# Four pairs of column groups as seven block products, spread over the head groups, the merge gates and the first branch

## The chip, the cores and the metric

The kernel runs on one core of one Trainium2 chip. The metric is the device time of one execution in microseconds (us), lower is better; three runs of the kernel before have a median of 1148.04 us.

## The reference

One decoder layer over 256 tokens of width 2048: a combined input projection, two token mixers side by side (gated linear attention, and differential attention with 16 heads), a gated merge of the two branches, and an output projection with a residual.

```python
h = rmsnorm(x, pre_norm_g)                       # x: (256, 2048)
(a_q, a_k, a_v, a_g, a_lr, b_q, b_k, b_v, b_g, m_a, m_b) = split(h @ w_in)
...
y_a = (rmsnorm(o_a, gla_norm_g) * silu(a_g)) @ w_branch_a      # gated linear attention
y_b = (rmsnorm(o_b, diff_norm_g) * 0.8 * silu(b_g)) @ w_branch_b   # differential attention
merged = sigmoid(m_a) * y_a + sigmoid(m_b) * y_b
out = x + rmsnorm(merged @ w_out, post_norm_g)
```

All of it is float32. b_g, m_a and m_b are 2048 columns each of the one wide matrix w_in.

## The kernel before

**Precision.** Every float32 weight and activation is split into two float32r parts, hi and lo. A product is three matmuls on TensorE (PE): hi by hi, lo by hi, hi by lo. ScalarE (ACT) makes hi, VectorE (DVE) makes lo.

**Chunks and units.** The weights are cut into chunks with keys: v, k, q, ag for the linear attention; dv, bg, dq, dk of head groups 0 to 3 (four heads each); m0g and m1g, the merge gates of the branches in groups of 512 columns; y0g and y1g, the branch products; o, the output. `chunk_plan` gives their order in DRAM. A token-major chunk of 512 columns has eight units of 128 x 1024 weights, a unit being twelve matmuls of 512 columns. A channel-major chunk (k, q, dq, dk) has two units. Two units come with one load of 1 MB into a `raw` tile (three buffers), issued on SyncE's queue (SP).

**The stream of units.** `schedule` writes out the order of all units. `emit_half` loads and splits the next unit (hi and lo have three buffers each), `take` hands one to the matmuls and keeps the emission AHEAD = 4 units in front. Side work (the attention of the heads, the preparation of operands) is written as generators that `pump` advances between units. A planner then orders each engine's instructions by their place in the program and by when it reckons them ready, and hands out buffers as they come free.

**Buffers.** The pool `big` has 34 tiles of 4 KB per partition, behind `u(...)`: xs (8, the split activations), oah/oal (8, the linear attention's output), per head group dv, ub, obh, obl and three tiles for each pair of heads, the merge gates (8). `t2` is a ring of eight tiles of 2 KB, PSUM has eight banks. `away` makes a DRAM tile.

**The sets.** m0 is not computed as four plain groups but as two sets. A set takes two groups of 512 columns as a 2 x 2 matrix of blocks and the tokens by halves of the width, and needs seven block products in place of eight (a form of Strassen's scheme). `PRODUCTS` lists them: the operand of the tokens, and the weight block that is loaded. Sums of weight blocks are made by the loads: two chains of four tiles each, a block loaded into a chain plainly first, and later ones added by an accumulating load issued on Pool's queue (GpSimd). Only the fourth product, a12, has its block unsummed; it goes through a `raw` tile (raw_s). `block_operands` makes the sums of the tokens' blocks, `start_sets` issues the first eight chain loads, and each emitted block issues the load of the one eight later (`load_block`). A block is six matmuls of 512 columns.

**Order before.** After the linear attention: heads 0, heads 1, y0 (its results, part, go to DRAM), heads 2, heads 3, then the stage in which the 56 blocks of the two sets run between the 32 units of m1, then y1, merge and o. obh and obl, the heads' results, go to DRAM as they are made and are reloaded with part ahead of y1 on SP's queue.

Of the kernel before, what the change touches and what calls it, by code (L numbers as in the profile page):

```python
# [30 lines left out]
def chunk_plan():  # L31
# [31 lines left out]

    heads(0)
    heads(1)
    for g in range(4):
        branch(0, g)
    heads(2)
    heads(3)
    for g in range(4):  # L70
        gate(1, g)
    for g in range(4):
        branch(1, g)
    for g in range(4):
        gate(0, g)
    for g in range(4):
# [8 lines left out]
def schedule():  # L85

    kinds = {key: kind for key, kind, _, _ in chunk_plan()}
    steps = []

    def regular(*keys):  # L90
        steps.extend((key, n) for key in keys for n in range(units(kinds[key])))

    def mixed(sets, *keys):
        s = [(i, n) for i in sets for n in range(SLOTS * 4)]
        at = len(steps)
        regular(*keys)
        r = steps[at:]
        del steps[at:]
        i = j = 0
        while i < len(s) or j < len(r):  # L100
            if j == len(r) or (i < len(s) and i * len(r) <= j * len(s)):
                steps.append(s[i])
                i += 1
            else:
                steps.append(r[j])
                j += 1

    order = [key for key, _, _, _ in chunk_plan()]
    first = order.index("m10")
    regular(*order[:first])  # L110
    mixed((0, 1), *(f"m1{g}" for g in range(4)))
    regular(*(f"y1{g}" for g in range(4)), *(f"o{g}" for g in range(4)))
    return steps


SLOTS = 7
SETS = (("m00", "m01"), ("m02", "m03"))

# [13 lines left out]
def hybrid_kernel(ctx: ExitStack, tc, xt, xn, preg, postg, w, w2, gkb, glag, lamv, diffg, ident_d, causal_d, lmask_d, out):  # L132
# [46 lines left out]
    raws = {}  # L179
    chains = [[], []]  # L180
    set_steps = [step for step in steps if not isinstance(step[0], str)]

# [15 lines left out]
    def load_block(i):  # L198
        if i < len(set_steps):
            chain, src, adds = block_unit(i)  # L200
            if adds:
                pool.dma_start(chain, src, accum_op=ALU.add)
            elif chain is not None:
                sp.dma_start(chain, src)

    def emit_half():
        j = emitted[0]
        emitted[0] += 1
        key, unit = steps[j]
        if isinstance(key, int):  # L210
            i = set_steps.index((key, unit))
            raw, src, _ = block_unit(i)
            if raw is None:
                h = unit % 2
                g = PRODUCTS[unit // 4][2][1]
                if h == 0:
                    kh = PRODUCTS[unit // 4][2][0]
                    raws[key] = wpool.tile([P, 2048], F32, tag="raw", name=f"raw_s{key}_{unit}")
                    sp.dma_start(raws[key], piece(SETS[key][g], 2 * kh + (unit % 4) // 2))
# [3 lines left out]
            act.activation(hi_t, raw, AF.Copy)  # L223
            dve.tensor_tensor(out=lo_t, in0=raw, in1=f32(hi_t), op=ALU.subtract)  # L224
            load_block(i + 8)
            ready[j] = ((key, unit), hi_t, lo_t)
            return
# [38 lines left out]
    used = [0]  # L266

    def take(key):
# [135 lines left out]
    def token_major(key, n, ops, step=1, groups=1):  # L404
        run = token_steps(key, n, ops, step, groups)
        while True:
            try:
                next(run)
            except StopIteration as e:
                return e.value  # L410

    def token_steps(key, n, ops, step=1, groups=1):
        banks = [[ps(tag), ps(tag)] for tag in ("mm", "bg")[:groups]]
        spots = [(g, b) for g in range(groups) for b in range(2)]
        rows = 2 // groups
        for q in range(KT // rows):
# [16 lines left out]
            if groups == 2 and q > 10:  # L433
                pump()
            if q < KT // rows - 1:
                yield
        return banks if groups == 2 else banks[0]
# [219 lines left out]
    oah = [u([P, 2, 2, S], "oah", F32R) for _ in range(4)]  # L657
    oal = [u([P, 2, 2, S], "oal", F32R) for _ in range(4)]

    def gla_out(hf, gates):  # L660
# [22 lines left out]
        for j in range(4):  # L683
# [41 lines left out]
    def diff_scores(g, pair, h, q2, kh, kl, vv, uu):  # L725
# [22 lines left out]
        return {"g": g, "pair": pair, "h": h, "z": z, "prob": prob, "vv": vv, "uu": uu}  # L748

# [23 lines left out]
    def normed(s, og):  # L773
# [10 lines left out]
        for b in range(2):  # L784
            dve.scalar_tensor_tensor(out=og[:, s["h"] % 2, b, :], in0=bank[:, P * b : P * b + P], scalar=e[:, b : b + 1], in1=s["uu"][:, b, hv], op0=ALU.mult, op1=ALU.mult)

    def diff_attention():
# [3 lines left out]
        while n < 16 or last or pair:  # L791
            new = None
            if n < 16:
# [8 lines left out]
                yield  # L802
                turn_weights(new)
            if last:
                weigh(last)
# [27 lines left out]

    def diff_heads(g, before_pair=lambda pair: None):
# [4 lines left out]
        banks = token_major(f"bg{g}", 512, x_ops, 2)  # L839
        uu = u([P, 2, 512], "ub")  # L840
        for b in range(2):
            gate(banks[b], b, uu[:, b, :])
        obh.append(u([P, 4, S], "obh", F32R))
        obl.append(u([P, 4, S], "obl", F32R))
        for pair in range(2):
            before_pair(pair)
            ts = []
# [58 lines left out]

    def start_sets():
        for c in range(2):
            chains[c].extend(u([P, 1024], f"chain{c}") for _ in range(4))
        for i in range(8):  # L910
            load_block(i)

    def block_set(n, use):
# [54 lines left out]
        yield  # L968

    tasks.append(diff_attention())  # L970
    diff_heads(0)
    diff_heads(1)

    while not {"out0", "out1"} <= done:
        pump()
    part_far = [away([P, 2, 512], "part_far") for _ in range(4)]
    for g in range(4):
        banks = token_major(f"y0{g}", 512, a_ops, 2)
        t = u([P, 2, 512], "part")
        for b in range(2):  # L980
            act.activation(t[:, b, :], banks[b], AF.Copy)
        pool.dma_start(part_far[g], t)

    diff_heads(2)
    operands = block_operands()
    tasks.append(operands)
    diff_heads(3, lambda pair: start_sets() if pair else None)

    while "squares" not in done:
        with tc.issue_after(latest[0]):  # L990
            next(operands, None)
    gates = [[None] * 4, [None] * 4]

    def merge_gate(br, g, b, src):
        if gates[br][g] is None:
            gates[br][g] = u([P, 2, 512], "mgate")
        act.activation(gates[br][g][:, b, :], src, AF.Tanh, scale=half_rstd[:, b : b + 1])

    def set_gates():
        for n in range(2):  # L1000
            yield from block_set(n, lambda src, i, b: merge_gate(0, 2 * n + i, b, src))

    def group_gates():
        for g in range(4):
            banks = yield from token_steps(f"m1{g}", 512, x_ops, 2)
            for b in range(2):
                merge_gate(1, g, b, banks[b])
            yield

    lanes = {True: set_gates(), False: group_gates()}  # L1010
    at = used[0]
    for key, _ in steps[at : at + 56 + 32]:
        next(lanes[isinstance(key, int)])
    for lane in lanes.values():
        assert next(lane, DONE) is DONE
    while tasks:
        pump()
    obh = [u([P, 4, S], "obh", F32R) for _ in range(4)]
    obl = [u([P, 4, S], "obl", F32R) for _ in range(4)]
    part = [u([P, 2, 512], "part") for _ in range(4)]  # L1020
    for g in range(4):
        sp.dma_start(f32(obh[g]), obh_far[g])
        sp.dma_start(f32(obl[g]), obl_far[g])
    for g in range(4):
        sp.dma_start(part[g], part_far[g])
    mh = [u([P, 4, S], "mh", F32R) for _ in range(4)]
    ml = [u([P, 4, S], "ml", F32R) for _ in range(4)]
# [156 lines left out]
```

## Time and profile before

| | before |
|---|---|
| median of 3 runs | 1148.04 us (1147.26 to 1149.27) |
| profiled execution, its own time | 1150.09 us |
| its span | 1148.3 us |
| PE busy | 1125.1 us, 98%, 5650 matmuls recorded |
| DVE, ACT, Pool busy | 748.3, 635.6, 84.1 us |
| moved by the DMA queues | 236.77 MB, 206 GB/s |

Times count from the start of the span. "Busy" is the time in which an engine executed; a matmul's recorded duration overlaps its successor's. In rows of the timeline the bracket gives the idle time ahead of an instruction and what ended it. "Granted clock" (PEclk) is the share of PE's full clock. The DMA share is the mean busy share of the core's 16 DMA engines; it can come out a little above 1. "SPq" is SyncE's queue, where loads are issued in order.

### The profile page before, as it was taken

What the parts mean: (1) busy time and instruction counts of PE and PEld (TensorE: products, weight loads), DVE (VectorE), ACT (ScalarE), POOL (GpSimd) and SP (SyncE); (2) the same over time, 40 slices, a digit from 0 to 9 for tenths busy, and PEclk for the clock granted to TensorE, in tenths of its full rate; (3) what the DMA queues carried; (4) which work ended last, traced back from release to release, by engine and by line L of the source; (5) the groups of instructions that cost most, each with busy time, mean ns of one, the idle gap of its engine ahead of it and who ended that gap; (6) DMA issues with size and microseconds to landing.
All of it is one profiled execution on the core that took longest, in us unless ns stands there. A gap on an engine that the chain in (4) does not pass through costs nothing.

```text
span 1148.3 us, 14907 instructions
## 1 busy us (share of the span) xinstructions
PE 1125.1 (98%) x5650; PEld 966.7 (84%) x5650; DVE 748.3 (65%) x1081; ACT 635.6 (55%) x942; POOL 84.1 (7%) x105
## 2 busy tenths in 40 slices
PE   9999999999999999999999999999899899999997
PEld 9999888888888888888888888888788787887886
DVE  6765587657847766775444677788677576655454
ACT  7675454445646665675444575477666464443441
POOL 0100031001100000000000010003112010000000
PEclk9999999999999999999999999999999899999999
DMA  8756555545454454456665555858899969657552
GB/s 310 228 191 220 184 177 176 196 167 195 141 175 168 151 180 155 177 187 221 221 215 183 184 187 180 307 188 226 254 304 262 257 183 365 209 195 257 187 216 74
DMA packets 41383, 236.77 MB, mean 206 GB/s; under 512 B 5152, under 2 KB 5792, under 8 KB 20320
## 3 DMA queue, kind: packets, MB, share of 16 engines
q1 hardware_dynamic: 34256, 211.70, 52.0%
q0 software_dynamic: 6336, 23.07, 9.1%
q10 hardware_dynamic: 720, 1.06, 0.3%
q8 instruction: 44, 0.72, 0.3%
q14 instruction: 27, 0.22, 0.1%
HBM read 227.42 MB, written 8.39 MB: 205 GB/s over the span
## 4 chain that ended last, share of the span: by engine, by line
PE 89%; DMA 3%; ACT 2%; DVE 2%; issue 2%; POOL 0%; SPq 0%; DVEq 0%; POOLq 0%; ACTq 0%
PE mm L426 55%; PE mm L449 15%; PE mm L451 7%; PE set L930 5%; PE bg L426 2%; DMA raw_m<-in_w_dram 1%; DMA raw_y<-in_w_dram 1%; PE mm L401 1%; PE bg L618 1%; ACT hi L262 1%; DVE lo L263 1%; PE bg L401 1%; PE bg L736 1%; DMA obl<-obl_far 1%; PE bg L737 1%
## 5 line engine op out<-in xcount | busy, mean ns | idle before, releaser
L426 PE MATMUL mm<-hi,xs 128*128 128x512 f32 (+2 forms) x1280 | 312.0, 385 | 7.5 <-ACT hi L262 7.5
L426 PEld LDWEIGHTS mm<-hi,xs 128*128 128x128 f32 x1280 | 239.7, 189 | 48.0 <-ACT hi L262 8.6
L449 PE MATMUL mm<-xs,hi 128*128 128x512 f32 x768 | 195.6, 393 | 0.0
L426 PE MATMUL mm<-lo,xs 128*128 128x512 f32 (+2 forms) x640 | 168.5, 383 | 0.0
L449 PEld LDWEIGHTS mm<-xs,hi 128*128 128x128 f32 x768 | 138.5, 189 | 24.2
L426 PEld LDWEIGHTS mm<-lo,xs 128*128 128x128 f32 x640 | 120.6, 189 | 20.8 <-DVE lo L263 0.3
L263 DVE TENSOR_TENSOR lo<-raw_y,hi 128x1024 fp32r<-128x1024 f32 x64 | 78.1, 1225 | 63.2 <-ACT hi L262 62.6
L262 ACT ACTIVATE hi<-raw_y 128x1024 fp32r<-128x1024 f32 x64 | 67.6, 1060 | 88.8 <-PE mm L426 77.3
L451 PEld LDWEIGHTS mm<-xs,lo 128*128 128x128 f32 x768 | 104.8, 190 | 7.5
L451 PE MATMUL mm<-xs,lo 128*128 128x256 f32 x768 | 107.1, 282 | 0.0
L224 DVE TENSOR_TENSOR lo<-chain,hi 128x1024 fp32r<-128x1024 f32 x48 | 58.6, 1223 | 17.8 <-ACT hi L223 17.1
L223 ACT ACTIVATE hi<-chain 128x1024 fp32r<-128x1024 f32 x48 | 50.8, 1061 | 27.9 <-PE set L930 19.4
L263 DVE TENSOR_TENSOR lo<-raw_bg,hi 128x1024 fp32r<-128x1024 f32 x32 | 39.2, 1224 | 30.8 <-ACT hi L262 30.8
L263 DVE TENSOR_TENSOR lo<-raw_ag,hi 128x1024 fp32r<-128x1024 f32 x32 | 41.2, 1289 | 27.2 <-ACT hi L262 27.2
L263 DVE TENSOR_TENSOR lo<-raw_m,hi 128x1024 fp32r<-128x1024 f32 x32 | 39.1, 1223 | 28.2 <-ACT hi L262 27.9
L262 ACT ACTIVATE hi<-raw_ag 128x1024 fp32r<-128x1024 f32 x32 | 33.8, 1060 | 42.4 <-PE mm L426 35.8
L262 ACT ACTIVATE hi<-raw_dq 128x1024 fp32r<-128x1024 f32 x32 | 34.0, 1061 | 41.7 <-PE mm L426 19.5
L263 DVE TENSOR_TENSOR lo<-raw_dq,hi 128x1024 fp32r<-128x1024 f32 x32 | 39.1, 1223 | 26.1 <-ACT hi L262 26.1
L262 ACT ACTIVATE hi<-raw_bg 128x1024 fp32r<-128x1024 f32 x32 | 33.9, 1060 | 38.8 <-PE mm L426 38.7
L263 DVE TENSOR_TENSOR lo<-raw_v,hi 128x832 fp32r<-128x832 f32 (+2 forms) x41 | 41.0, 1015 | 20.5 <-ACT hi L262 20.2
L263 DVE TENSOR_TENSOR lo<-raw_dk,hi 128x1024 fp32r<-128x1024 f32 x32 | 39.2, 1224 | 22.3 <-ACT hi L262 22.0
L262 ACT ACTIVATE hi<-raw_dk 128x1024 fp32r<-128x1024 f32 x32 | 33.9, 1060 | 35.3 <-PE mm L449 34.2
(255 smaller groups left out, 1964.0 us busy)
## 6 DMA issues: line engine op xcount, KB each, us to landing
raw_y<-in_w_dram SPq DMA_DIRECT2D x32, 1024.0 KB, 4.9
raw_ag<-in_w_dram SPq DMA_DIRECT2D x16, 1024.0 KB, 4.8
raw_dv<-in_w_dram SPq DMA_DIRECT2D x16, 1024.0 KB, 4.8
raw_bg<-in_w_dram SPq DMA_DIRECT2D x16, 1024.0 KB, 4.8
raw_dq<-in_w_dram SPq DMA_DIRECT2D x16, 1024.0 KB, 4.9
raw_dk<-in_w_dram SPq DMA_DIRECT2D x16, 1024.0 KB, 4.9
raw_m<-in_w_dram SPq DMA_DIRECT2D x16, 1024.0 KB, 7.4
chain<-in_w_dram POOLq DMA_DIRECT2D x32, 512.0 KB, 10.9
```

The lines of the kernel that those rows point to most:

```text
L223: act.activation(hi_t, raw, AF.Copy)
L224: dve.tensor_tensor(out=lo_t, in0=raw, in1=f32(hi_t), op=ALU.subtract)
L262: act.activation(hi_t[:, a:b], r, AF.Copy)
L263: dve.tensor_tensor(out=lo_t[:, a:b], in0=r, in1=f32(hi_t[:, a:b]), op=ALU.subtract)
L401: i = pe.matmul(out, lhs, rhs, start=first and n == 0, stop=last and n == len(pairs) - 1)
L426: i = pe.matmul(banks[g][b][:, :n], a[part][:, P * b : P * b + P], w[:, c : c + n], start=first, stop=last)
L449: i = pe.matmul(o, hi[:, c], x_pair(kt), start=kt == 0, stop=kt == KT - 1)
L451: i = pe.matmul(o[:, :S], lo[:, c], x_ops(kt)[0], start=False, stop=False)
L618: pe.matmul(o, xk[:, P * c : P * c + P], xq.rearrange("p (b c t) -> p b c t", b=2, c=4)[:, :, c, :], start=i == 0, stop=i == 1)
L736: pe.matmul(banks[m][:, lo:up], q2[:, m, i2, t], kh[:, m, i2, :n], start=True, stop=False)
L737: pe.matmul(banks[m][:, lo:up], q2[:, m, i2, t], kl[:, m, i2, :n], start=False, stop=True)
L930: i = pe.matmul(bank, a[part], wt[:, 512 * j : 512 * j + 512], start=go, stop=end, skip_group_check=not first)
```

## The change

Two more sets are made: bg2 with bg3, and m10 with m11. The 112 blocks of the four sets are spread between the plain units from the channels of heads 1 to the end of y0: 16 with heads 1's channels, 20 with dv2 and heads 2's, 20 with dv3 and heads 3's, 20 with m12 and m13, 36 with y0, which now stands behind the heads and the gates. All chain loads go out on Pool's queue, six blocks ahead in place of eight. In the third and fourth set one of the sums (product n2) is made by DVE from the other chain in place of an accumulating load. The operands of the sets are prepared ahead of heads 1; whatever is left of them is issued when `start_sets` is called, seven steps before the first block. oah and oal, and the merge gates, go to DRAM and are reloaded. The gate of heads 2 and 3 comes out of the first set (`late_gates`).

```diff
-    heads(0)
-    heads(1)
     for g in range(4):
-        branch(0, g)
...
+        heads(g)
+    for br, g in ((1, 2), (1, 3), (1, 0), (1, 1), (0, 0), (0, 1), (0, 2), (0, 3)):
+        gate(br, g)
+    for br in range(2):
+        for g in range(4):
+            branch(br, g)
...
+    blocks = [(i, n) for i in range(len(SETS)) for n in range(SLOTS * 4)]
...
+    def mixed(n, *keys):
...
+        for i, step in enumerate(r):
+            steps.extend(blocks[: (i + 1) * n // len(r) - i * n // len(r)])
+            del blocks[: (i + 1) * n // len(r) - i * n // len(r)]
+            steps.append(step)
...
-    mixed((0, 1), *(f"m1{g}" for g in range(4)))
+    regular(*order[: order.index("dq10")])
+    mixed(16, *channels(1))
+    mixed(20, "dv2", *channels(2))
+    mixed(20, "dv3", *channels(3))
+    mixed(20, "m12", "m13")
+    mixed(36, *(f"y0{g}" for g in range(4)))
...
-SETS = (("m00", "m01"), ("m02", "m03"))
+SETS = (("bg2", "bg3"), ("m10", "m11"), ("m00", "m01"), ("m02", "m03"))
+
+DVE_SUMS = 2
...
@@ load_block
-            if adds:
+            n, step = set_steps[i]
+            if n >= DVE_SUMS and step // 4 == 4:
+                dve.tensor_tensor(out=chain, in0=chain, in1=chains[(n + 1) % 2][step % 4], op=ALU.add)
+            elif adds:
                 pool.dma_start(chain, src, accum_op=ALU.add)
             elif chain is not None:
-                sp.dma_start(chain, src)
+                pool.dma_start(chain, src)
@@ emit_half
+        if j == first_set - 7:
+            start_sets()
...
-            load_block(i + 8)
+            load_block(i + 6)
@@ take
+        while isinstance(key, str) and not isinstance(steps[used[0]][0], str):
+            next(blocks[0])
@@ gla_out
+                pool.dma_start(oah_far[i], f32(oah[i]))
+                pool.dma_start(oal_far[i], f32(oal[i]))
@@ diff_attention
+            while last and last["uu"] is None and last["g"] - 2 not in late_gates:
+                yield
@@ start_sets
+        while "squares" not in done:
+            with tc.issue_after(latest[0]):
+                next(operands, None)
...
-        for i in range(8):
+        for i in range(6):
             load_block(i)
...
+    def merge_gate(br, g, b, src):
+        t = t2([P, 512], "mgate")
+        act.activation(t, src, AF.Tanh, scale=half_rstd[:, b : b + 1])
+        pool.dma_start(gates_far[g][br][b], t)
...
+    diff_heads(0)
     while not {"out0", "out1"} <= done:
         pump()
...
     operands = block_operands()
     tasks.append(operands)
...
+    blocks[0] = all_sets()
+    diff_heads(1)
+    diff_heads(2)
+    diff_heads(3)
+
+    for g in (2, 3):
+        banks = token_major(f"m1{g}", 512, x_ops, 2)
+        for b in range(2):
+            merge_gate(1, g, b, banks[b])
     while tasks:
         pump()
+    oah = [u([P, 2, 2, S], "oah", F32R) for _ in range(4)]
+    oal = [u([P, 2, 2, S], "oal", F32R) for _ in range(4)]
+    for i in range(4):
+        sp.dma_start(f32(oah[i]), oah_far[i])
+        sp.dma_start(f32(oal[i]), oal_far[i])
+    for g in range(4):
+        banks = token_major(f"y0{g}", 512, a_ops)
...
+            pool.dma_start(part_far[g][:, b, :], t)
...
     for g in range(4):
         sp.dma_start(part[g], part_far[g])
+        for br in range(2):
+            for b in range(2):
+                sp.dma_start(gates[br][g][:, b, :], gates_far[g][br][b])
...
     for g in range(4):
+        dve.scalar_tensor_tensor(out=part[g], in0=gates[0][g], scalar=1.0, in1=part[g], op0=ALU.add, op1=ALU.mult)
         banks = token_major(f"y1{g}", 512, b_ops)
-        dve.scalar_tensor_tensor(out=part[g], in0=gates[0][g], scalar=1.0, in1=part[g], op0=ALU.add, op1=ALU.mult)
```

More of the change, by code (lines that the diff above doesn't have):

```diff
@@ L98, in mixed, with channels @@
         del steps[at:]
[L99 to L106, printed above, removed]
-    order = [key for key, _, _, _ in chunk_plan()]
-    first = order.index("m10")
-    regular(*order[:first])
-    mixed((0, 1), *(f"m1{g}" for g in range(4)))
+        for i, step in enumerate(r):
+            steps.extend(blocks[: (i + 1) * n // len(r) - i * n // len(r)])
+            del blocks[: (i + 1) * n // len(r) - i * n // len(r)]
+            steps.append(step)
+    def channels(g):
+        return [key for key in kinds if key[:2] in ("dq", "dk") and key[2] == str(g)]
+    order = [key for key, _, _, _ in chunk_plan()]
+    regular(*order[: order.index("dq10")])
[4 more added lines that the diff above has]
+    mixed(36, *(f"y0{g}" for g in range(4)))
     regular(*(f"y1{g}" for g in range(4)), *(f"o{g}" for g in range(4)))
+    assert not blocks
     return steps
 SLOTS = 7
-SETS = (("m00", "m01"), ("m02", "m03"))
+SETS = (("bg2", "bg3"), ("m10", "m11"), ("m00", "m01"), ("m02", "m03"))
+DVE_SUMS = 2
 PRODUCTS = (
@@ L180, in hybrid_kernel @@
     chains = [[], []]
+    first_set = next(j for j, step in enumerate(steps) if not isinstance(step[0], str))
     set_steps = [step for step in steps if not isinstance(step[0], str)]
@@ L658, in hybrid_kernel @@
     oal = [u([P, 2, 2, S], "oal", F32R) for _ in range(4)]
+    oah_far = [away([P, 2, 2, S], "oah_far") for _ in range(4)]
+    oal_far = [away([P, 2, 2, S], "oal_far") for _ in range(4)]
     def gla_out(hf, gates):
@@ L832, in diff_attention, with gate_of_set, diff_heads @@
                 yield
-    def diff_heads(g, before_pair=lambda pair: None):
+    late_gates = {}
+    def gate_of_set(src, i, b):
+        if i not in late_gates:
+            late_gates[i] = u([P, 2, 512], "ub")
+        gate(src, b, late_gates[i][:, b, :])
+    def diff_heads(g):
         banks = token_major(f"dv{g}", 512, x_ops, 2)
@@ L838, in diff_heads @@
             act.activation(vv[:, b, :], banks[b], AF.Copy, scale=rstd[:, b : b + 1])
[L839 to L842, printed above, removed]
+        uu = None
+        if g < 2:
+            banks = token_major(f"bg{g}", 512, x_ops, 2)
+            uu = u([P, 2, 512], "ub")
+            for b in range(2):
+                gate(banks[b], b, uu[:, b, :])
         obh.append(u([P, 4, S], "obh", F32R))
@@ L989, in hybrid_kernel @@
[L989 to L1015, printed above, removed]
+    blocks[0] = all_sets()
+    diff_heads(1)
@@ L1020, in hybrid_kernel @@
     part = [u([P, 2, 512], "part") for _ in range(4)]
+    gates = [[u([P, 2, 512], "mgate") for _ in range(4)] for _ in range(2)]
     for g in range(4):
@@ L1025, in hybrid_kernel @@
         sp.dma_start(part[g], part_far[g])
+        for br in range(2):
+            for b in range(2):
+                sp.dma_start(gates[br][g][:, b, :], gates_far[g][br][b])
     mh = [u([P, 4, S], "mh", F32R) for _ in range(4)]
```

47 lines of the change are left out of this document (15 added, 32 removed).

## The prediction

> **What bounds the kernel now.** I read the head of the page first, then PE's idle stretches in the timeline, then the chain of waits, the stretches and SyncE's queue around them.
>
> ```profile
> span 1148.3 us, 14907 instructions
> ...
> PE 1125.1 (98%) x5650; PEld 966.7 (84%) x5650; DVE 748.3 (65%) x1081; ACT 635.6 (55%) x942; POOL 84.1 (7%) x105
> ...
> PE   9999999999999999999999999999899899999997
> ...
> DMA  8756555545454454456665555858899969657552
> ...
> q1 hardware_dynamic: 34256, 211.70, 52.0%
> q0 software_dynamic: 6336, 23.07, 9.1%
> ```
>
> PE is busy 1125.1 of 1148.3 us, so the end is set by the amount of matmul work and by the few places where PE stops. The profiled execution took 1150.09 us (1.8 us outside its span) and the runs shown have a median of 1148.04; every sum below is a difference, taken off 1148.04. The transfers are no bound on average (52.0% + 9.1%), but the slices from 26 on show nines, so the stages have to be read one by one.
>
> ```profile
> core 0: us, PE busy (x) PEld busy (x) DVE busy (x) ACT busy (x) POOL busy (x), PEclk, DMA share, GB/s
> 390.00:434.00 44.00, 44.00 (x223) 37.15 (x222) 29.28 (x59) 28.20 (x51) 1.84 (x3) 1.00 0.47 162
> 757.00:785.00 28.00, 27.15 (x157) 23.42 (x156) 24.76 (x51) 21.88 (x47) 5.69 (x8) 1.00 0.55 144
> 772.00:954.00 182.00, 174.25 (x782) 143.37 (x781) 125.92 (x158) 117.78 (x158) 33.42 (x41) 0.98 0.87 242
> 785.00:820.00 35.00, 34.99 (x163) 28.94 (x162) 26.04 (x54) 24.16 (x42) 9.31 (x12) 1.00 1.05 270
> 860.00:900.00 40.00, 40.00 (x178) 33.14 (x177) 27.97 (x24) 25.19 (x27) 10.52 (x12) 1.00 1.01 262
> 950.00:975.00 25.00, 22.57 (x97) 17.77 (x96) 15.11 (x14) 9.97 (x11) 0.00 (x0) 1.00 1.01 407
> ```
>
> The stage in which the two sets of block products run beside the m1 groups (772 to 954 us) loses 182.0 - 174.25 = 7.75 us of PE, at a DMA share of 0.87, with stretches above 1.0. The individual stops stand in the timeline of PE (the bracket is the idle time and what ended it): those of the head groups before it (497 and 682 us), then those of the set stage:
>
> ```profile
> 497.16 0.33 PE L736 MATMUL bg<-kh,q 128*128 128x128 f32 x1 [0.35 <-ACT kh L717]
> ```
>
> ```profile
> 681.92 0.33 PE L736 MATMUL bg<-kh,q 128*128 128x128 f32 x1 [0.38 <-ACT kh L717]
> ```
>
> ```profile
> 783.34 0.33 PE L736 MATMUL bg<-kh,q 128*128 128x128 f32 x1 [0.69 <-ACT kh L717]
> ...
> 823.75 2.14 PE L426 MATMUL mm<-hi,xs 128*128 128x512 f32 x8 [3.30 <-ACT hi L262]
> ```
>
> ```profile
> 911.99 3.78 PE L426 MATMUL mm<-hi,xs 128*128 128x512 f32 x8 [3.60 <-ACT hi L262]
> ...
> 955.49 0.70 PE L426 MATMUL mm<-hi,obh 128*128 128x512 f32 x2 [1.04 <-ACT hi L262]
> 956.66 0.74 PE L426 MATMUL mm<-hi,obl 128*128 128x512 f32 x2 [0.47 <-DMA obl<-obl_far]
> ...
> 973.75 0.50 PE L426 MATMUL mm<-hi,obh 128*128 128x512 f32 x1 [0.91 <-ACT hi L262]
> ```
>
> The chain of waits says what stood behind the two large ones:
>
> ```profile
> 786.94 2.72 PE mm L426 x12
> ...
> 815.37 7.19 DMA raw_m<-in_w_dram
> ...
> 823.75 3.06 PE mm L426 x12
> 826.81 1.36 PE set L930 x6
> ...
> 901.71 9.09 DMA raw_m<-in_w_dram
> ...
> 911.99 5.49 PE mm L426 x12
> 917.48 1.60 PE set L930 x6
> ```
>
> Twelve 512-column matmuls are 2.72 us at the full clock, 0.2267 us each, and six are 1.36. Both large stops end on a weight transfer (7.19 and 9.09 us). After the stop of 3.60 us the next twelve and six matmuls took 5.49 and 1.60 us, which is 2.77 + 0.24 = 3.01 lost to a lower clock; after the one of 3.30 us only 3.06 - 2.72 = 0.34. Together the two cost 3.30 + 0.34 + 3.60 + 3.01 = 10.25 us, 5.13 for each set.
>
> ```profile
> 777.94 0.33 SPq L241 DMA_DIRECT2D raw_m<-in_w_dram  x1
> 791.66 8.86 SPq L219 DMA_DIRECT2D raw_s<-in_w_dram  x2
> 815.37 24.25 SPq L241 DMA_DIRECT2D raw_m<-in_w_dram  x5
> ...
> 949.56 0.42 SPq L1022 DMA_DIRECT2D obh<-obh_far  x1
> ...
> 955.41 4.05 SPq L1025 DMA_DIRECT2D part<-part_far  x4
> ```
>
> SyncE's queue names the mechanism. A set's fourth product (a12) is the one whose weights are not summed: its two raw_s tiles take two of the three raw buffers (791.66), so the next raw_m can go only when an older tile is split (815.37), with PE about to need it. At the far end of the stage come twelve reloads in a row (obh, obl, part; 949.56 to 959.5) and behind them the y1 weights: 1.04 + 0.47 + 0.91 = 2.42 us of stops.
>
> **The change part by part.**
>
> *Two more sets (bg2/bg3 and m10/m11).* A pair of plain 512-column groups is 2 x 96 = 192 matmuls on PE, a set 7 x 24 = 168. So 2 x 24 = 48 fewer, 48 x 0.2267 = **-10.9 us**. PE is the path; nothing else hides here. Everything else is a question of waits.
>
> *Spreading the sets.* Per plain unit there were 56/32 = 1.75 blocks; there will be 1.0, 0.83, 0.83, 1.25 and 1.125 in the five stretches. Around a12 four blocks and their plain units last 4 x 1.36 + (4/r) x 2.72: 11.7 us before; 16.3, 18.5, 14.1 and 15.1 us for the four sets. In that time they ask for 2 raw_s and 2/r raw tiles, 3.1 before, 3.6 to 4.4 now; one tile per 3.7 us before, per 3.9 to 4.2 now. The next raw tile is still issued only when one of the three is free, so the wait does not vanish; it has somewhat more time to land, and it meets fewer neighbours:
>
> ```profile
> raw_y<-in_w_dram SPq DMA_DIRECT2D x32, 1024.0 KB, 4.9
> ...
> raw_m<-in_w_dram SPq DMA_DIRECT2D x16, 1024.0 KB, 7.4
> chain<-in_w_dram POOLq DMA_DIRECT2D x32, 512.0 KB, 10.9
> ```
>
> A raw tile lands in 7.4 us in the set stage and 4.9 elsewhere. Bounds for a set: nothing (if the 4.9 us hold) and 5.13 us as now. I take 1.5, nearer to the low end since the tiles are further apart, and a shorter stop than 3.30 us brings the smaller clock loss. So **-10.25 us** for the two places that go and 4 x 1.5 = **+6** (0 to 20.5) for the four that come.
>
> *Bandwidth.* From the queue rows, q1's 211.70 MB at 52.0% of 1148.3 us is 355 GB/s at full share. Of q0's 23.07 MB the 32 accumulating loads of 512 KB are 16.8 MB; the rest at q1's rate takes 18 us of its 104, leaving 86 us, 2.7 us for one accumulated block against 1.5 for a plain one. After the change 56 blocks are accumulated (sets two and three add one product on DVE instead) and 32 are loaded plainly on Pool's queue; oah, oal and the sixteen gate tiles go to DRAM and back. I reckon 262 MB, q0 at about 61 MB, and a mean share near 0.71. The densest stretch is y0 (600 matmuls, 136 us): 14 accumulated x 2.7, 12 other block loads and 32 weight units x 1.5, and about 29 us of other transfers (part 6, gates 5, obh and obl 12, the first y1 weights 6), 133 us in all. That is a share of 0.98, more than the 0.87 of the old set stage, whose stops were not at its densest slices alone. **+2 us** (0 to 10.25, what the old stage lost).
>
> *The operands and the first loads.* They start seven steps before the first block, that is with the emission of bg1, and what is left of them then is issued in one go.
>
> ```profile
> L224 DVE TENSOR_TENSOR lo<-chain,hi 128x1024 fp32r<-128x1024 f32 x48 | 58.6, 1223 | 17.8 <-ACT hi L223 17.1
> L223 ACT ACTIVATE hi<-chain 128x1024 fp32r<-128x1024 f32 x48 | 50.8, 1061 | 27.9 <-PE set L930 19.4 <-PE mm L426 7.1 <-ACT hi L262 0.8
> ...
> L202 POOL DMA_DIRECT2D chain<-in_w_dram x32 | 28.2, 880 | 160.7 <-DVE lo L224 152.2 <-DVE de L780 5.2 <-DVE mx L742 2.0
> ...
> L889 DVE TENSOR_TENSOR full_a<-xs 128x256 f32<-128x256 f32 x16 | 6.0, 418 | 0.0
> ...
> L895 DVE TENSOR_TENSOR full_a<-full_a,full_a 128x1024 f32<-128x1024 f32 x4 | 4.9, 1222 | 0.1
> ...
> L822 POOL DMA_DIRECT2D obh_far<-obh x4 | 2.5, 625 | 10.8 <-ACT obh L461 9.2 <-ACT junkd L778 1.5
> ...
> L901 DVE TENSOR_TENSOR lo_s<-full_a,hi_s 128x1024 fp32r<-128x1024 f32 x2 | 2.4, 1222 | 1.0 <-ACT hi_s L900 1.0
> L901 DVE TENSOR_TENSOR lo_n<-full_a,hi_n 128x1024 fp32r<-128x1024 f32 x2 | 2.4, 1219 | 0.0
> ```
>
> The operands are 6.0 + 4.9 + 2.4 + 2.4 = 15.7 us of DVE. In dv1 and bg1 (390 to 434) DVE now works 29.28 of 44 us; with them 45.0, more than the stretch has. PE holds about two and a half units of 2.72 us in store (three hi and lo buffers), 6.8 us. Bounds: 0, since half of it can slide under the first channels before the second product needs it, and since 757 to 785 held DVE at 24.76 of 28 us with only 0.85 us lost; and 15.7 - 6.8 = 8.9. I take **+3 us**.
>
> *DVE and ACT in the head groups.* A block costs DVE 1.22 and ACT 1.06 us for 1.36 us of PE, a plain unit the same for 2.72. A head group gains 20 blocks and loses the 8 units of its gate group: 12 x 1.22 = 14.6 us of DVE, spread. The eight DVE sums (1.22 us each) are 9.8 us over 140 us. Covered by the slack of DVE outside the first stretch; 0, up to 6 if the attention's bursts meet them.
>
> *Pool's queue.* 88 chain issues instead of 32 and 28 more stores: 56 x 0.88 + 28 x 0.6 = 66 us more of Pool, 150 in all, 13%. What waits behind a chain issue is the rsqrt of the attention and DVE behind that, 0.88 us for each issue ahead; the attention's results are not due until y1. What it frees: SyncE's queue no longer has chain loads between the weight loads. 0 either way.
>
> *Turn to y1.* oah/oal are reloaded when the attention's buffers come free, in m12/m13 (cover: 71 us of PE). obh/obl can follow while set three gives up its operands. What falls on the first y1 group is part (2.1 MB) and the gates (4.2), 6.3 MB, the same as obh, obl and part before. The 2.42 us stay: 0 (from -2.4 to +3, if a part product that now stands ahead of its y1 group holds up DVE for a reload).
>
> Sum: -10.9 - 10.25 + 6 + 2 + 3 = **-10.2 us: 1137.8**, in the profile 1139.9. I say **1137.5**.
>
> [...]
>
> **The rivals.**
>
> *All waits hidden.* The tiles land in 4.9 us, the burst slides: 1148.04 - 10.9 - 10.25 = 1126.9, and 1124.5 if the stops before y1 go as well. For it: before the set stage PE loses under half a us per head group (0.35, 0.38). Against it: three raw buffers as before.
>
> *Other side: each of the four sets stops PE as each of the two does now.* Place: the raw tile behind a12. 4 x 5.13 = 20.5 instead of 6: 1148.04 - 10.9 - 10.25 + 20.5 + 5 = 1152.4. It decides from 4.6 us a set on ((10.9 + 10.25 - 5 + 2.3) / 4). For it: same buffers, more traffic elsewhere. Against: fewer blocks per unit, and in the last two sets half of the accumulated loads behind a12 are gone. [...]
>
> *The heads run out of tiles.* xs, the operands and the chains hold 24 of the 34 large buffers from group 1 on; ten are left for a group that uses about ten. Then a split waits for the pair before, and PE for the split, as at 783.34 (0.69 us). Six pairs; at 0.69 each +4.1, 1141.9; slower from 2.1 us a pair on ((10.2 + 2.3) / 6), 1150.4; with the 3.60 and 3.01 us of the worst stop each, 1177.5. Against it: the attention's own pace, one head for two chunks, frees a pair's tiles before the next pair's are due.
>
> **How the numbers follow.** Forecast, waits of this kind and size (1130 to 1145.7): 0.57. All hidden (below 1130): 0.20. Four stops of old size: 0.16, half of that within 0.2%, half beyond. Heads out of tiles, past their point: 0.07. So faster 0.77, same 0.08, slower 0.15; 0.2% (2.3 us) is about what a measurement of this kernel can tell from none. The range 1125 to 1147 leaves out the slower cases and a little below.
>
> **What would show it.** PE's instruction count down by 48 and its busy time near 1112; DVE near 787 us; 262 MB, q0 near 61. In PE's timeline: stops of 1 to 2 us on a raw tile at four places, one of about 3 us near 410 to 430 on lo behind full_a, none over 3.4. Wrong would be: stops above 4.6 us at the four a12, a lower granted clock in the heads, PE waiting on kh, or in y0 a row of waits on raw_y.

## The result, and the profile after

The changed kernel takes 1141.6 us (median of 5 runs, 1141.49 to 1145.04) against 1149.23 before; the ratio is 0.9941, with a 95% interval of 0.9922 to 0.9961. So it is faster by 0.6%, where 0.9% was forecast; the time lies in the range, 4.1 us above the likeliest value. The profiled execution took 1141.49 us, its span 1139.7, which is 8.6 us shorter.

From the page of the changed kernel: totals, DMA slices and queues.

```profile
span 1139.7 us, 15092 instructions
...
PE 1110.5 (97%) x5602; PEld 954.5 (84%) x5602; DVE 788.7 (69%) x1125; ACT 659.3 (58%) x970; POOL 142.3 (12%) x189
...
DMA  8756554545465387988688887869998996557552
...
q1 hardware_dynamic: 33680, 199.12, 48.7%
q0 software_dynamic: 16896, 60.83, 21.7%
```

48 matmuls fewer, PE busy 14.6 us less (10.9 of it the matmuls), DVE up by 40 us, q0 at 60.83 MB: the amounts came out as reckoned. PE's idle time however rose, from 1148.3 - 1125.1 = 23.2 to 1139.7 - 1110.5 = 29.2 us. Where it lies, first in the head groups, from the timeline of PE:

```profile
429.36 0.30 PE L766 MATMUL bg<-ident,prob 128*128 128x128 f32 x1 [0.32 <-DVE prob L761]
...
438.35 0.30 PE L766 MATMUL bg<-ident,prob 128*128 128x128 f32 x1 [1.64 <-ACT hi L229]
...
523.97 0.33 PE L740 MATMUL bg<-kh,q 128*128 128x128 f32 x1 [1.10 <-ACT kh L721]
```

and then in y0 (each stop with, for the first two, the row after its twelve matmuls):

```profile
813.00 0.71 PE L428 MATMUL mm<-hi,oah 128*128 128x512 f32 x1 [3.48 <-ACT hi L268]
...
817.43 0.39 PE L947 MATMUL set<-hi,hi_n 128*128 128x512 f32 x1
...
894.52 0.50 PE L428 MATMUL mm<-hi,oah 128*128 128x512 f32 x1 [3.49 <-ACT hi L268]
...
898.97 1.09 PE L947 MATMUL set<-hi,xs 128*128 128x512 f32 x4
...
927.59 1.20 PE L428 MATMUL mm<-lo,oah 128*128 128x512 f32 x4 [3.50 <-DVE lo L269]
```

Three stops of 3.5 us are 10.47 us, all inside y0 (801 to 950 us). After the first two, twelve matmuls took 817.43 - 813.00 = 4.43 and 898.97 - 894.52 = 4.45 us in place of 2.72, another 1.71 and 1.73. What stood behind them is in the timelines of ACT and of DVE:

```profile
811.89 1.06 ACT L268 ACTIVATE hi<-raw_y 128x1024 fp32r<-128x1024 f32 x1 [7.62 <-DMA raw_y<-in_w_dram]
...
893.42 1.06 ACT L268 ACTIVATE hi<-raw_y 128x1024 fp32r<-128x1024 f32 x1 [6.23 <-DMA raw_y<-in_w_dram]
```

```profile
917.11 1.23 DVE L230 TENSOR_TENSOR lo<-chain,hi 128x1024 fp32r<-128x1024 f32 x1 [0.99 <-ACT hi L229]
925.17 1.22 DVE L1060 SCALAR_TENSOR_TENSOR part<-mgate,part 128x1024 f32<-128x1024 f32 x1 [6.84 <-DMA mgate<-gate_far]
926.32 1.22 DVE L269 TENSOR_TENSOR lo<-raw_y,hi 128x1024 fp32r<-128x1024 f32 x1
```

The first two wait for a tile of y0's weights. The third is of another kind: DVE stands for 6.84 us at the product of part with its gate (L1060) because the gate's reload has not landed, and the split that PE needs (926.32) is queued behind it. The stretches, in the columns that the prediction showed:

```profile
390.00:434.00 44.00, 42.97 (x216) 35.68 (x215) 40.84 (x88) 30.99 (x56) 9.42 (x15) 1.00 0.76 281
...
730.00:805.00 75.00, 75.00 (x361) 62.68 (x360) 57.28 (x89) 50.67 (x82) 18.74 (x25) 1.00 0.88 271
805.00:960.00 155.00, 144.53 (x621) 118.34 (x621) 94.67 (x85) 81.15 (x85) 21.64 (x32) 0.98 0.91 301
813.00:823.00 10.00, 10.00 (x37) 8.14 (x38) 8.63 (x9) 5.96 (x7) 1.29 (x3) 0.83 1.02 423
927.50:937.50 10.00, 9.91 (x44) 8.21 (x45) 8.95 (x11) 5.67 (x6) 0.00 (x0) 1.00 0.73 239
```

m1 runs at a DMA share of 0.88 and loses nothing; in y0 (805 to 960) PE loses 155.0 - 144.53 = 10.47 us at a share of 0.91. The stops before the first y1 group (2.42 us before) are gone: obh and obl were reloaded during y0.

### The profile page after: what moved, and what is told of

Its sections match the earlier page's. It is cut to its first block, busy times and chain, and to the rows that moved or that the text cites. A ratio compares the mean times of both kernels' runs of the same rounds, so it can differ in the third digit from the quotient of the medians.

```text
span 1139.7 us, 15092 instructions
## 1 busy us (share of the span) xinstructions
PE 1110.5 (97%) x5602; PEld 954.5 (84%) x5602; DVE 788.7 (69%) x1125; ACT 659.3 (58%) x970; POOL 142.3 (12%) x189
## 2 busy tenths in 40 slices
DMA packets 51370, 261.97 MB, mean 230 GB/s; under 512 B 6432, under 2 KB 7072, under 8 KB 31840
## 3 DMA queue, kind: packets, MB, share of 16 engines
q0 software_dynamic: 16896, 60.83, 21.7%
## 5 line engine op out<-in xcount | busy, mean ns | idle before, releaser
L428 PE MATMUL mm<-hi,xs 128*128 128x512 f32 (+2 forms) x1024 | 246.6, 381 | 2.0 <-ACT hi L268 2.0
L428 PEld LDWEIGHTS mm<-hi,xs 128*128 128x128 f32 x1024 | 189.9, 188 | 31.8 <-ACT hi L268 2.5
L230 DVE TENSOR_TENSOR lo<-chain,hi 128x1024 fp32r<-128x1024 f32 x96 | 117.5, 1224 | 53.8 <-ACT hi L229 52.5
L229 ACT ACTIVATE hi<-chain 128x1024 fp32r<-128x1024 f32 x96 | 101.7, 1060 | 90.4 <-PE mm L428 33.3
L206 POOL DMA_DIRECT2D chain<-in_w_dram x56 | 49.8, 890 | 237.1 <-DVE lo L230 140.7
L428 PE MATMUL mm<-hi,oah 128*128 128x512 f32 x128 | 51.7, 404 | 7.0 <-ACT hi L268 7.0
L947 PE MATMUL set<-hi,xs 128*128 128x512 f32 x192 | 52.1, 393 | 0.0
L428 PE MATMUL mm<-hi,oal 128*128 128x512 f32 x128 | 51.5, 403 | 0.0
L428 PE MATMUL mm<-hi,obh 128*128 128x512 f32 x128 | 50.1, 391 | 0.0
L428 PE MATMUL mm<-hi,obl 128*128 128x512 f32 x128 | 49.8, 389 | 0.0
```

What stands on the lines that cost most here:

```text
L428: i = pe.matmul(banks[g][b][:, :n], a[part][:, P * b : P * b + P], w[:, c : c + n], start=first, stop=last)
L947: i = pe.matmul(bank, a[part], wt[:, 512 * j : 512 * j + 512], start=go, stop=end, skip_group_check=not first)
```

## The experiments

Theory: the three stops have three causes, the reload of oah and oal, the fourth set's unsummed product a12, and the product on DVE. Rival: y0 is short of transfer rate as a whole, and a stop taken away comes back elsewhere. Each ratio below is to the kernel before, run beside it on the same chip. Its median lay between 1148.84 and 1149.69 us there; the changed kernel's own differed more (1141.6 and 1145.03 us), so a small difference between times from two chips says little.

**The changed kernel once more.**

> The changed kernel unaltered, so that the next three stand beside it on the same chip. Both theories: about 1141.6 us, three stops of PE of 3.5 us in y0 (near 810, 891 and 924 us), 10.5 us together, the first two followed by 1.7 us at a lower clock.

Measured: 1145.03 us, 0.9957 [0.9941, 0.9972]. The same three stops, the first of 2.44 us. It is the control for the next three runs; its spread (1141.46 to 1147.50) is taken up at the end.

**The product's line moved back.**

```diff
-        dve.scalar_tensor_tensor(out=part[g], in0=gates[0][g], ...)
         banks = token_major(f"y1{g}", 512, b_ops)
+        dve.scalar_tensor_tensor(out=part[g], in0=gates[0][g], ...)
```

> One line of the change undone: the product of the gates with part stands behind the matmuls of its y1 group again. Theory (three stops with three causes: the reload of oah and oal, the unsummed product of the fourth set, and DVE held by this product while its gate is still on the way): the third stop, on lo, goes and nothing else, 3.8 us less than the control, about 1137.8. Rival (the y0 stage is short of transfer rate as a whole, so a stop that is taken away comes back elsewhere in it): the same as the control within 1 us, with a new stop on a weight tile.

Measured: 1145.53 us, 0.9965 [0.9949, 0.9981], the same as the control. The theory's gain did not come, and yet the run does not speak for the rival: the edit did not do what it was meant to do. All three stops are there (2.43, 5.19 and 2.95 us; the profiled execution, 1149.44 us, is one of the longest of twelve). On DVE the product still stands between the splits of y0 and still waits for the gate:

```profile
928.61 1.23 DVE L1061 SCALAR_TENSOR_TENSOR part<-mgate,part 128x1024 f32<-128x1024 f32 x1 [6.29 <-DMA mgate<-gate_far]
```

The planner places an instruction by when it reckons its inputs ready, so the line's place in the program had not made the stop.

**Without the reload of oah and oal.**

```diff
-    for i in range(4):
-        sp.dma_start(f32(oah[i]), oah_far[i])
-        sp.dma_start(f32(oal[i]), oal_far[i])
-        banks = token_major(f"y0{g}", 512, a_ops)
+        banks = token_major(f"y0{g}", 512, x_ops)
```

> Leaves out the reload of oah and oal: y0 takes the split activations as its operand instead, with the same matmuls. 4.2 MB less ahead of y0, and eight large buffers that are free earlier. Theory: the first stop (3.48 us and 1.71 us of lower clock) goes, the other two stay or move by little: 5.2 us less, about 1136.4. Rival: the rate is short all through y0, so the 4.2 MB (12 us of all transfer engines) help the second stop too: 8 to 10 us less.

Measured: 1142.43 us, 0.9942 [0.9928, 0.9957], 2.6 us less than the control where 5.2 or 8 to 10 were expected. In PE's timeline the stop at 813 is gone and the second stays, but a new one of 4.78 us has come, and DVE's timeline shows it to be the product again, earlier, as the reload of the first gate was issued at 848 us in place of 879:

```profile
857.21 1.22 PE L947 MATMUL set<-lo,hi_s 128*128 128x512 f32 x2 [4.78 <-DVE lo L230]
...
897.33 2.93 PE L428 MATMUL mm<-hi,xs 128*128 128x512 f32 x7 [3.94 <-ACT hi L268]
```

```profile
854.79 1.23 DVE L1055 SCALAR_TENSOR_TENSOR part<-mgate,part 128x1024 f32<-128x1024 f32 x1 [8.17 <-DMA mgate<-gate_far]
```

So the first stop needs the reload, and the third moves with the planner's order. The second did not shrink (3.94 us), against the rival.

**The reloads of part and gates in y1.**

```diff
-    for g in range(4):
-        sp.dma_start(part[g], part_far[g])           # and the gates of g
...
     for g in range(4):
-        dve.scalar_tensor_tensor(out=part[g], in0=gates[0][g], ...)
+        late = tc.keep_in_program_order
+        late(sp.dma_start(part[g], part_far[g]))     # and the gates of g
         banks = token_major(f"y1{g}", 512, b_ops)
+        dve.scalar_tensor_tensor(out=part[g], in0=gates[0][g], ...)
```

> The reloads of part and of the gates are pinned group by group behind the weights of their y1 group, and the product behind its matmuls: 6.3 MB leave the y0 stage. Theory: the third stop goes as in the run with the product behind, and the second (3.49 and 1.73 us) if reloads in SyncE's queue were what held up its weight tile: 3.8 to 9 us less, 1132.6 to 1137.8, and no new stop in y1, where the DMA share is 0.63. Rival: the second stop is the fourth set's unsummed product alone and stays: 3.8 us less.

Measured: 1137.4 us, 0.9898 [0.988, 0.9915], 7.6 us less than the control and 4.2 less than the changed kernel's first runs. The third stop is gone and nothing new came in y1; the other two are as in the control (2.38 and 3.48 us), which is the rival's case for the second. The time falls by more than the rival's 3.8 us; in the control's profile the third stop (3.39 us) was followed by a granted clock of 0.69 over 10 us, which is another 3.1. (The first group's reloads still went out in y0, at 878 us: the pin is behind what SyncE's queue already held.)

**Four raw buffers in the kernel before.**

```diff
-    big = ctx.enter_context(tc.tile_pool(name="big", bufs=34))
+    big = ctx.enter_context(tc.tile_pool(name="big", bufs=32))
-            raws[key] = wpool.tile([P, 2048], F32, tag="raw", ...)
+            raws[key] = wpool.tile([P, 2048], F32, tag="raw", ..., bufs=4)
```

> The kernel before with four raw buffers in place of three (and 32 large buffers in place of 34). Theory (a set's unsummed product takes two of three raw buffers, so the next weight tile is issued too late): the two stops of 3.30 and 3.60 us at 823 and 912 us go with their clock loss, up to 10.2 us less, about 1139 to 1142. Rival (the set stage was short of transfer rate, and more tiles in flight only queue): stops of the same size, 1149.

Measured: 1135.9 us, 0.989 [0.9874, 0.9905]: 13.0 us less, more than the whole change brought. Both stops of the old set stage are gone. The same stretch in the kernel before and in this run:

```profile
805.00:940.00 135.00, 128.09 (x568) 105.22 (x567) 88.84 (x100) 83.25 (x104) 21.71 (x26) 0.97 0.93 260
```

```profile
805.00:940.00 135.00, 135.00 (x608) 111.74 (x607) 97.54 (x109) 89.39 (x108) 21.71 (x26) 1.00 0.93 264
```

PE lost 6.91 us of it before and nothing now, at the same DMA share of 0.93. So a share this high did not make the stops by itself; the missing buffer did. Of the 2.8 us beyond the theory's 10.2, about 1.5 are the clock behind the last merge (1.00 in this profile, 0.83 in the one before, see the end) and 0.9 a stop fewer at the turn to y1.

**The chain loads on Pool's queue, in the kernel before.**

```diff
-                sp.dma_start(chain, src)
+                pool.dma_start(chain, src)
-            load_block(i + 8)
+            load_block(i + 6)
```

> One part of the change alone in the kernel before: the plain chain loads go out on Pool's queue, six blocks ahead. Theory: SyncE's queue was not what held the weights up at the unsummed product (its chain loads stood elsewhere, at 841 to 863 us), so both stops stay, 1149 within 2 us. Rival: with nothing of the chains in SyncE's queue the weight tiles go out earlier and the stops shrink, 4 us less or more.

Measured: 1149.7 us, 1.0004 [0.9995, 1.0014]. Both stops stay, within 0.05 us; this part of the change is worth nothing by itself in the kernel before.

```profile
822.93 3.35 PE L426 MATMUL mm<-hi,xs 128*128 128x512 f32 x7 [3.34 <-ACT hi L262]
...
913.91 3.67 PE L426 MATMUL mm<-hi,xs 128*128 128x512 f32 x8 [3.65 <-ACT hi L262]
```

**Plain loads in the last two sets.**

```diff
-                pool.dma_start(chain, src, accum_op=ALU.add)
+                pool.dma_start(chain, src, accum_op=ALU.add if n < DVE_SUMS else ALU.bypass)
```

> The changed kernel with the accumulating loads of the third and fourth set made plain; leaves out those sums. 24 loads of 512 KB at about 1.5 in place of 2.7 us of all transfer engines. Theory of rate (the second stop comes from the loads that bunch behind the fourth set's unsummed product): the second stop goes or falls below 1.5 us, the third (DVE waiting for a gate) stays: 3 to 5 us less than the changed kernel, 1138 to 1141 beside 1144. Rival (the raw buffers alone make it): the second stop stays within 1 us.

Measured: 1130.15 us, 0.9836 [0.9818, 0.9853], 11.4 us less than the changed kernel's first runs, far more than the theory gave. All three stops shrink, to nothing, 0.36 and 0.47 us, with the same bytes moved:

```profile
888.32 0.50 PE L428 MATMUL mm<-hi,oah 128*128 128x512 f32 x1 [0.36 <-ACT hi L268]
...
916.75 1.19 PE L428 MATMUL mm<-lo,oah 128*128 128x512 f32 x4 [0.47 <-DVE lo L269]
```

```profile
q0 software_dynamic: 16896, 60.83, 19.1%
```

q0's time falls from 21.7% of 1139.7 to 19.1% of 1128.9 us, 31.7 us for 24 loads: 1.3 us each, close to the 2.7 - 1.5 of the prediction. So this run's own rival, buffers alone, is out, and the rival of the whole section gains: the time that accumulating loads take from the transfer engines in m1 and y0 has a part in all three stops. (A plain load also costs Pool less to issue, 0.55 in place of 0.89 us on average in the changed kernel's profile, so the run does not change the rate alone.)

**Blocks spread evenly, with the late reloads.**

```diff
-    mixed(20, "dv2", *channels(2))
-    mixed(20, "dv3", *channels(3))
-    mixed(20, "m12", "m13")
-    mixed(36, *(f"y0{g}" for g in range(4)))
+    mixed(24, "dv2", *channels(2))
+    mixed(24, "dv3", *channels(3))
+    mixed(24, "m12", "m13")
+    mixed(24, *(f"y0{g}" for g in range(4)))
```

> The reloads pinned in y1 as in the run before, and the blocks spread 16, 24, 24, 24, 24 in place of 16, 20, 20, 20, 36: y0 has 24 blocks in 32 units. Theory (y0 is the stretch that is short of rate): the stops at 813 and 894 us fall to under half (from 2.4 and 3.5 us), for 1 to 2 us more of waits in the heads: 1132 to 1135. Rival (the stop moves with the block): the same sum of stops at other places, 1137.5 as with the late reloads alone, or more where DVE gets dense in the heads.

Measured: 1138.93 us, 0.9913 [0.9897, 0.993], not better than the late reloads alone (0.9898). The stop at 894 broke up, the one at the start of y0 stayed at 2.29, and a new one stands in m1:

```profile
759.70 2.11 PE L428 MATMUL mm<-hi,xs 128*128 128x512 f32 x8 [1.59 <-ACT hi L268]
...
837.65 0.50 PE L428 MATMUL mm<-hi,oah 128*128 128x512 f32 x1 [2.29 <-ACT hi L268]
...
875.41 1.20 PE L947 MATMUL set<-hi,xs 128*128 128x512 f32 x4 [0.73 <-ACT hi L229]
```

With two small ones behind the last (0.64 and 0.46 us) the stops in m1 and y0 are 5.7 us together, against 2.38 + 3.48 = 5.9 with the late reloads alone. They moved with the blocks; the rival's case.

**The unsummed block in buffers of its own, with the late reloads.**

```diff
+            if raw is None and key >= FAR_SETS:          # FAR_SETS = 2
...
+                raw = u([P, 1024], f"raw_s{key}_{unit}")
+                sp.dma_start(raw, piece(...)[:, 1024 * h : 1024 * h + 1024])
```

> The late reloads, and the unsummed product of the third and fourth set is loaded into four large buffers of its own in place of two raw tiles, so that the three raw buffers hold weights of plain units alone. Theory of buffers (the raw tiles are what a set's unsummed product takes from the plain units, as four raw buffers showed in the kernel before): the stop at 894 us (3.48) goes, the one at 813 (2.4) stays: 4 to 5 us less than the late reloads alone, 1132 to 1134. Rival of rate (the accumulating loads of y0 are what is too much): the stop stays within 1 us, 1137.

Measured: 1133.09 us, 0.9864 [0.9844, 0.9884], in the band of the theory of buffers, though in part by luck: 4.3 us less than the late reloads alone, whose interval it just touches. Both weight stops are gone, the first too, which was not expected: the third set's unsummed product stands just ahead of y0, and without it in the raw tiles the last of m1's weights were issued at 766 us in place of 780. Against that a stop of 2.33 us came that no side named, again with the product in front on DVE, waiting for the first group's gate:

```profile
895.27 1.23 DVE L1066 SCALAR_TENSOR_TENSOR part<-mgate,part 128x1024 f32<-128x1024 f32 x1 [5.71 <-DMA mgate<-gate_far]
```

**The last sum of the last two sets on DVE.** The four tiles are kept, since the last product adds the same block.

```diff
+            elif n >= FAR_SETS and step // 4 == 6:
+                dve.tensor_tensor(out=chain, in0=chain, in1=kept.pop((n, step % 4)), op=ALU.add)
             elif adds:
                 pool.dma_start(chain, src, accum_op=ALU.add)
```

> The same, and these four tiles are kept: the last sum of the third and fourth set adds the very block that the unsummed product used, so DVE adds it from there and eight accumulating loads of 512 KB (2.7 us of all transfer engines each) fall away, for eight sums of 1.22 us on DVE. Theory of rate: both stops in y0 (813 and 894 us) under 1 us, PE idle 5 to 6 us less than with the late reloads alone, 1128 to 1131. Theory of buffers: as the run before it, 1132 to 1134. Rival: the four tiles, held longer, keep back the reload of oah, obh or the attention: a new stop of over 2 us at the start of y0 or y1, 1136 or more.

Measured: 1128.57 us, 0.9818 [0.9799, 0.9837], 13 us less than the changed kernel's first runs, 4.5 less than the run before it, and the lowest ratio of all runs, as the theory of rate gave. PE is not idle once between 805 and 960 us, at a share of 0.84:

```profile
805.00:960.00 155.00, 155.00 (x685) 128.34 (x685) 109.53 (x98) 87.33 (x91) 17.95 (x28) 1.00 0.84 286
```

**The product pinned**, in the changed kernel and in the one just told.

```diff
-        dve.scalar_tensor_tensor(out=part[g], in0=gates[0][g], ...)
+        tc.keep_in_program_order(dve.scalar_tensor_tensor(out=part[g], in0=gates[0][g], ...))
         banks = token_major(f"y1{g}", 512, b_ops)
```

> The changed kernel, the product of the gates with part pinned on DVE behind the splits of the first units of its y1 group, so that its place on the engine does change (moving the line alone had left it where it was). Theory: the third stop (3.50 us and 0.3 to 3 us of lower clock) goes, the first two stay: 3.8 to 6 us less than the changed kernel, 1138 to 1140. Rival (rate as a whole): a stop of 2 to 3.5 us on a weight tile takes its place, 1143 to 1145.

Measured: 1139.32 us, 0.9911 [0.9885, 0.9936], in the theory's band against 0.9941 and 0.9957 for the changed kernel; its interval overlaps that of the first runs and ends just below the control's. The trace is plain: the third stop is gone, and the other two stay (2.84 and 3.79 us), with none on a weight tile in its place.

```profile
814.83 0.50 PE L428 MATMUL mm<-hi,oah 128*128 128x512 f32 x1 [2.84 <-ACT hi L268]
...
896.69 0.50 PE L428 MATMUL mm<-hi,oah 128*128 128x512 f32 x1 [3.79 <-ACT hi L268]
```

> The kernel with the last sums of the third and fourth set on DVE and late reloads, and the product pinned as well. There DVE waited 2.4 us for a gate without stopping PE: the same within 1.5 us, 1127 to 1130. Rival: the pinned product comes too late for the merge of its group, and PE waits for it at the end of y1: 1 to 3 us more.

Measured: 1128.09 us, 0.9827 [0.9807, 0.9848], the same as without the pin.

Two combinations were not run: four raw buffers in the changed kernel, and plain loads in place of the accumulating ones in the old set stage. As far as the runs go, a stop on a weight tile needs both a load that lands late and too few buffers to issue it early; taking away either left 0.36 us of it at most.

## Why the prediction was right, and where its sizes were off

- *Matmuls, -10.9 us*: right. 5602 in place of 5650, with no other change of PE's work.
- *The two old stops, -10.25*: right, and the mechanism with it. They went with the spreading, and one more raw buffer takes them out of the kernel before at the same DMA share.
- *Four new stops behind a12, +6*: the first three sets have none, the fourth has one of 3.49 + 1.73 = 5.2 us, the full price of an old one (5.13). The sum came near by luck: no set showed the stop of 1.5 us that was forecast. That the distance between tiles sufficed for the first three is likely, but no run shows it.
- *Rate in y0, +2*: too small. The first stop alone is 3.48 + 1.71 = 5.2 us. The share of 0.98 was worked out nearly rightly (133 us of transfers forecast, 0.91 of 155 = 141 measured) and then discounted. The split between this term and the one before is loose: plain loads take out both stops, and so do buffers of their own for the unsummed product.
- *Operands, +3*: 0.32 and 1.64 us near 430, so 2.0, with DVE at 40.84 of 44 us (45.0 forecast). The place was another than forecast: nothing stopped behind full_a (the operands were done by 422 us), and the 1.64 us ended on the hi of a block, which ACT could make only after attention work that had waited for DVE. A stop of 0.71 us at 393 us lies ahead of the operands (they start at 401 us): PE waits there for ua, part of the linear attention, which the changed kernel finishes before it begins the operands. No term priced it.
- *DVE and ACT in the heads, 0*: small waits for the attention's splits, 1.10 us at most; with the others in the heads 2.4, against 1.6 before.
- *Turn to y1, 0*: two effects that nearly cancelled. The 2.42 us went, since obh and obl came early; and the product held up DVE, which cost PE 3.8 us (3.50 of idle time, 3.79 counted from matmul start to matmul start), the case that stood in brackets at +3. The reason given for it (the line moved ahead of the group) was wrong, as the moved line and then the pin show: it is the planner's order, which a pin can change.

The terms by their measured sizes: -10.9 - 10.25 + 5.2 + 5.2 + 2.0 + 0.7 + 0.8 - 2.42 + 3.8 = -5.9 us, against -7.6 in the medians and -8.6 in the span. Some 1.5 of the rest is the clock behind the last merge, told below. Another 0.7 lies ahead of 186 us, in work that both kernels share (ACT's first split of raw_ag starts at 185.2 in place of 185.9). About 0.5 us of the span is not assigned.

Of the signs that the prediction named, the amounts came: 48 matmuls fewer, PE at 1110.5 us for 1112, DVE at 788.7 for 787, 261.97 MB for 262. The stops of 1 to 2 us at four places did not, and in place of none over 3.4 us there are three of 3.5. Waits on raw_y in y0, one of its signs of being wrong, came twice. So the gains were right; the waits came to 15.3 us in place of 11, and most of them lay elsewhere than forecast.

Of the rivals, that the heads run out of tiles did not show (PE's longest wait there was 1.10 us), and that each set stops PE at the old price held for one set of four. The traffic elsewhere, which the other side had for it, shows in y0, where a weight tile took up to 24.7 us to land (13.3 in the kernel before):

```profile
L247 SPq DMA_DIRECT2D raw_y<-in_w_dram x32: 327/332/439, 779.9 to 1016.4; - x32
...
DMA to landing us min/median/max: 4.7/6.6/24.7
```

This is the tile of the first stop, issued at 787.1 us right behind six reloads of oah and oal in SyncE's own queue. In the run without these reloads that stop is gone; with plain loads in the last two sets, which keeps them, it is gone too, and the longest tile took 15.6 us. So no run separates a shortage of rate from waiting behind the queue's own reloads.

## What to carry to other kernels

Before work is spread to keep loads apart, ask what a stop waits for: in the kernel before one more buffer for the raw weights brought more (13.0 us) than two more sets with all their transfers (7.6). Price an accumulating load by the engine time it takes (2.7 against 1.5 us here, both estimates from the queue rows; 1.3 us of difference in the run with plain loads), not by its bytes, and take the sum to an engine with time to spare where the block is in memory anyway. A high share over a stage is a warning, not yet a cost: at 0.93 PE lost 6.91 us of 135 with three raw buffers and nothing with four. And where a planner orders the engines, an instruction that waits for a reload has to be pinned, not moved in the text.

## What the runs showed of the hardware

The loss after a stop is not fixed by its length. In the changed kernel the stop of 3.50 us at 927.59 was followed by the full clock (the stretch from 927.5 above, 1.00), in its second profile one of 3.39 us by 0.69; and there one of 2.44 us was followed by 0.83.

```profile
812.13 0.50 PE L428 MATMUL mm<-hi,oah 128*128 128x512 f32 x1 [2.44 <-ACT hi L268]
...
926.65 2.07 PE L428 MATMUL mm<-lo,oah 128*128 128x512 f32 x4 [3.39 <-DVE lo L269]
```

```profile
812.10:822.10 10.00, 9.97 (x37) 8.07 (x38) 8.61 (x9) 5.91 (x7) 1.20 (x3) 0.83 1.03 417
926.60:936.60 10.00, 9.95 (x31) 7.96 (x32) 6.28 (x6) 4.06 (x4) 0.00 (x0) 0.69 0.67 239
```

That a stop shorter than 3.30 us brings the smaller clock loss was the prediction's estimate from two stops (0.34 us lost after 3.30 us, 3.01 after 3.60). The 2.44 us disagree, since 0.83 over 10 us is a loss of 1.7; so does the stop of 2.38 us at the end of y1, after which the granted clock was 0.83 in the kernel before and 1.00 in the changed one:

```profile
1049.80:1059.80 10.00, 9.95 (x41) 8.28 (x42) 4.98 (x6) 3.31 (x4) 0.00 (x0) 0.83 1.00 374
```

```profile
1042.60:1052.60 10.00, 9.92 (x48) 8.35 (x49) 5.39 (x7) 4.21 (x5) 0.00 (x0) 1.00 1.01 390
```

So stops of equal length ended differently here (2.38 us, at 0.83 and at 1.00). Whether this makes the spread of the times is not shown: seven runs of the changed kernel spread over 6 us (1141.46 to 1147.50) and four with plain loads, almost without stops in y0, over 2.3 (1129.05 to 1131.37), but five of the kernel without any stop in y0 (last sums on DVE) again over 4.8 (1126.45 to 1131.23).
